# Activation slices of 256 words instead of 272, each tile starting 48 words into its place

## The chip, the core and the metric

The kernel runs on one core of a Trainium2 chip. The core has a matrix engine (TensorE: PE in the profile, with its weight loads listed apart as PEld), a vector engine (DVE), a scalar engine (ACT), GpSimd (POOL) and a queue engine (SP) that issues most of the DMAs. The metric is the device time of one execution in microseconds, as the median of several runs. TensorE's granted clock has two levels, 1.2 and 2.4 GHz, which the profile gives as a share (1.00 is 2.4 GHz).

## The reference

Two transformer-like blocks over 256 tokens of width 1024, in float32. Cut to the large products that matter here:

```python
# first block, 256 tokens
z = rmsnorm(x, g) @ w_in                     # q, k, mq, u (feature-major), v, f, gate (token-major)
x = x + rmsnorm(concat(gmlp, fox, memory) @ w_out, g2)
f = square(relu(rmsnorm(x, g3) @ w_ff1)) @ w_ff2          # 1024 -> 4096 -> 1024
x = x + rmsnorm(f, g4)
# second block, 16 meta tokens + 256 tokens
proj = rmsnorm(h) @ w_in_2                   # z, xbc, dt, conf
h = h + concat(y_ssd, y_conf) @ w_out_2
xt = rmsnorm(h, g5)                          # PEER: 16384 experts
q = xt @ w_query                             # top-16 experts of 8 heads per token
act = gelu(einsum("td,thkd->thk", xt, w_down[experts])) * gate
h = h + einsum("thk,thkd->td", act, w_up[experts])
```

## The kernel before

**Products.** A float32 product is made of three matmuls. `load_split` (line 198) brings a 512 KB piece of weights into `wf` (128 partitions by 1024 words, a DMA on SP's queue), ACT rounds it to `wh` (line 217), and DVE writes the rest, `wl = wf - wh` (line 218). There are four `wf` buffers and three each of `wh` and `wl`. The activations are split in the same way into a pair `..h`, `..l`. `mm3` (lines 221 to 224) then issues, for a weight slice of 128 words and an activation slice:

```python
matmul(o, wh, ah)    # L222
matmul(o, wh, al)    # L223
matmul(o, wl, ah)    # L224
```

In `proj_fm`, `proj_fm_k` and the stage called S below, the weight slice is the stationary operand (128 columns, loaded by PEld), and the activation slice is the moving operand: 256 words, one for each token. While a moving operand streams, PEld loads the weights of the next matmul.

**Where the activations lie.** `act_pair` (line 383) hands out a pair from two places that the whole program shares, tags `acth` and `actl`. It lays a tile out as 8 slices (one for each 128 features) of 272 words, because one stage (`u`, 16 meta tokens and 256 tokens) needs 272; the other stages use the first 256 words of each slice:

- `hh, hl` (line 418): the input of the first block. Moving in the products `qk` and `u` (264 matmuls of 256 words); stationary in the first, token-major product (96 matmuls), in which the weights move.
- `h2h, h2l` (line 772): the input of `w_ff1`, 768 matmuls. They come in 8 groups of 96: 8 slices, and 12 matmuls for each slice. Between two such groups stand 96 matmuls of `w_ff2`, whose activations `fah, fal` come from another pool, with slices of 256 words.
- `uh, ul` (line 882): 272 words, the only user that asks for TM.
- `os1h, os1l` (line 1174): four slices of `w_out_2`'s input, 96 matmuls, 24 for each slice.
- `xth, xtl` (line 1287): the input of the stage S (`w_down`, PEER's first product): 128 steps, each of one 512 KB piece of weights, 8 slices, 3 matmuls for each slice: 3,072 matmuls.

**Addresses.** The built program puts `acth` at byte 61984 and `actl` at 70688 of each partition, the `wh` buffers at 37408, 41504 and 45600, the `wl` buffers at 49696, 53792 and 57888. All six weight buffers start at the same place modulo 512 bytes, and their slices are 512 bytes (128 words) apart. In this document the *distance* of an activation slice is its address minus that of a weight slice, in words, modulo 128. For a user of `act_pair` slice k has the distance 16k: 0, 16, 32, 48, 64, 80, 96, 112, and the `l` tile has the same distances as the `h` tile. `fah, fal` and `os0h, os0l` have 112 in every slice, `xuh, xul` (the input of `w_query`, products `q`) 64 in every slice.

**What sets the order.** The Python order of the code, with generators (`ch`, `bg`) that put attention, selection and gate work between the weight pieces by a budget of estimated microseconds. While S runs, DVE selects the experts (`select`, budget 1.21 for each piece), POOL scatters the gates of the first 128 tokens to DRAM (`scatter`, line 1350, 128 indirect DMAs) and reads them back (line 1522), and later PE puts the gates of the other 128 tokens between S's steps (products `pg`, line 1476). The last stage, `acc` (line 1568, 1,536 matmuls with 512 moving words), uses no `act_pair` tile; DVE's first use of the gates that POOL read back is line 1507.

Of the kernel before, what the change touches and what calls it, by code (L numbers as in the profile page):

```python
# [8 lines left out]
F32R = mybir.dt.float32r  # L9
# [7 lines left out]
P = 128  # L17
T = 256
TM = 272
# [50 lines left out]
LN_WAIT = 1.5, 3.0  # L70

LAST = 3

UP_EARLY = 2

# [83 lines left out]
def tile_two_blocks(ctx: ExitStack, tc: tile.TileContext, A, out):  # L159
# [221 lines left out]
    act = ctx.enter_context(tc.tile_pool(name="act", bufs=1))  # L381

    def act_pair(name, t):
        h = act.tile([P, 8, TM], F32R, name=f"{name}h", tag="acth")
        l = act.tile([P, 8, TM], F32R, name=f"{name}l", tag="actl")
        return h[:, :, :t], l[:, :, :t]

    sres = ExitStack()
    resid = sres.enter_context(tc.tile_pool(name="resid", bufs=1))
# [26 lines left out]

    m0 = xp.tile([P, 8, T], F32, name="m0", tag="x1")
    hh, hl = act_pair("h", T)
    sq = ap.tile([P, 8, T], F32, name="sq", tag="sq")
    mh = ap.tile([P, 8, T], F32R, name="mh")  # L420
# [291 lines left out]
    for k0 in range(0, 8, 2):  # L712
        wh, wl = load_split(A["w_kv"][:, k0:k0 + 2, :], [P, 2, 512])
        for j in range(2):
            k = k0 + j
# [21 lines left out]
    def add_normed(bs, gain, src, dst, eps, name, pool, tmp, then):  # L737

        with tc.high_priority(offset=PRIO):
# [21 lines left out]
            for m in range(8):  # L761
# [8 lines left out]
    assert not zero_parts  # L770
    x1 = xp.tile([P, 8, T], F32, name="x1", tag="x1")
    h2h, h2l = act_pair("h2", T)
    add_normed(bs, "post_mix", x0, x1, eps1, "pm", xp, tp,
               lambda m: split_to(h2h[:, m, :], h2l[:, m, :], x1[:, m, :], col("pre_ffn", m)))
# [16 lines left out]
    for r in range(4):  # L791
        for g in range(4):
            o = _COL["ccw"]
# [55 lines left out]
    for g in range(9):  # L849
# [21 lines left out]
        if g >= 1:  # L871
            ah, al = held[g - 1]
            for j in range(4):
                k = (g - 1) * 4 + j
# [5 lines left out]
                bg.run(BUDGET["diag"])  # L880
    bg.drain()
    uh, ul = act_pair("u", TM)

    split_to(uh[:, :, 0:NM], ul[:, :, 0:NM], meq)
# [632 lines left out]
    for i in range(0, P, 2):  # L1517
# [13 lines left out]
        n = state["toks"]  # L1531
# [20 lines left out]
    for i in range(P):  # L1552
# [11 lines left out]
        def products(t, fs, i=i, ah=ah, al=al, wh=wh, wl=wl):  # L1564
            c = slice(t * P, (t + 1) * P)
            for l, w, e in ((ah, wh, False), (ah, wl, False), (al, wh, i == P - 1)):
                for f in fs:
                    nc.tensor.matmul(acc[t][f], l[:, c], w[:, f * 512:(f + 1) * 512], start=False, stop=e,  # L1568
                                     skip_group_check=True)

        products(0, (0, 1))
        if i >= P - LAST:
            late.append(products)
# [111 lines left out]
```

## Time and profile before

| | us |
|---|---|
| median of 3 runs | 1368.78 |
| lowest and highest run | 1365.6, 1371.24 |
| the profiled execution, whole time | 1370.11 |
| the profiled execution, its span | 1368.4 |

The span is the time from the first to the last instruction of the profile; 1.7 us of the execution lie outside it. PE is busy in 99% of the span, but a busy PE is not a PE at its peak: matmuls overlap, and what counts is the distance in time between the starts of two of them. A matmul of 256 moving words is listed with some 280 ns, while the next one starts some 118 ns later. So the views that matter are the timeline of PE, read by start times, and the list of waits, for what else could hold PE up.

### The profile page before, as it was taken

What the parts mean: (1) busy time and instruction counts of PE and PEld (TensorE: products, weight loads), DVE (VectorE), ACT (ScalarE), POOL (GpSimd) and SP (SyncE); (2) the same over time, 40 slices, a digit from 0 to 9 for tenths busy, and PEclk for the clock granted to TensorE, in tenths of its full rate; (3) what the DMA queues carried; (4) which work ended last, traced back from release to release, by engine and by line L of the source; (5) the groups of instructions that cost most, each with busy time, mean ns of one, the idle gap of its engine ahead of it and who ended that gap; (6) DMA issues with size and microseconds to landing.
All of it is one profiled execution on the core that took longest, in us unless ns stands there. A gap on an engine that the chain in (4) does not pass through costs nothing.

```text
span 1368.4 us, 25834 instructions
## 1 busy us (share of the span) xinstructions
PE 1350.3 (99%) x10054; PEld 1255.6 (92%) x10054; DVE 985.9 (72%) x1924; ACT 756.3 (55%) x1263; POOL 307.1 (22%) x223
## 2 busy tenths in 40 slices
PE   9999999999999999999999999999999999999998
PEld 8988899999888899999999999999998888888886
DVE  6985777657637896798989976666666666666665
ACT  6665444445334675654544548787755555555454
POOL 3122200000310000000048888888600000000000
PEclk9999999999999999999999999999999999999999
DMA  8466666663663343645668776666666777677764
GB/s 297 141 220 226 185 185 189 194 189 113 202 195 107 108 141 109 200 143 165 185 184 186 186 186 156 159 151 158 172 201 220 212 224 220 216 218 214 221 210 131
DMA packets 120730, 250.45 MB, mean 183 GB/s; under 512 B 28048, under 2 KB 52368, under 8 KB 120480
## 3 DMA queue, kind: packets, MB, share of 16 engines
q1 hardware_dynamic: 97328, 235.89, 56.3%
q0 software_dynamic: 22704, 12.35, 6.3%
q8 instruction: 79, 1.29, 0.4%
q10 hardware_dynamic: 576, 0.57, 0.1%
q14 instruction: 43, 0.35, 0.1%
HBM read 234.60 MB, written 9.50 MB: 178 GB/s over the span
## 4 chain that ended last, share of the span: by engine, by line
PE 93%; DVE 3%; DMA 2%; ACT 1%; issue 1%; POOL 0%; SPq 0%; DVEq 0%; ACTq 0%; POOLq 0%
PE acc L1568 25%; PE S L224 9%; PE S L223 9%; PE S L222 9%; PE ff L222 4%; PE ff L223 4%; PE ff L224 4%; PE pg L1476 2%; PE cv L922 2%; PE wo L222 2%; PE wo L224 2%; PE wo L223 2%; PE cf L222 1%; PE cf L224 1%; PE cf L223 1%; PE q L223 1%
## 5 line engine op out<-in xcount | busy, mean ns | idle before, releaser
L218 DVE TENSOR_TENSOR wl<-wf,wh 128x1024 fp32r<-128x1024 f32 (+1 forms) x425 | 515.7, 1215 | 234.7 <-ACT wh L217 234.1
L217 ACT CAST wh<-wf 128x1024 fp32r<-128x1024 f32 (+1 forms) x425 | 442.8, 1043 | 377.9 <-PE S L223 145.4
L222 PE MATMUL S<-xth,wh 128*128 128x256 f32 x1024 | 289.6, 283 | 0.0
L223 PE MATMUL S<-xtl,wh 128*128 128x256 f32 x1024 | 288.6, 282 | 0.0
L224 PE MATMUL S<-xth,wl 128*128 128x256 f32 x1024 | 288.3, 282 | 0.0
L1350 POOL DMA_INDIRECT G<-small x128 | 241.9, 1890 | 163.4 <-DVE small L1344 124.7
L224 PEld LDWEIGHTS S<-xth,wl 128*128 128x128 f32 x1024 | 194.2, 190 | 0.0
L222 PEld LDWEIGHTS S<-xth,wh 128*128 128x128 f32 x1024 | 193.8, 189 | 0.0
L223 PEld LDWEIGHTS S<-xtl,wh 128*128 128x128 f32 x1024 | 192.5, 188 | 0.0
L1568 PE MATMUL acc<-wh,ah 128*128 128x512 f32 x512 | 158.3, 389 | 0.0
L1568 PE MATMUL acc<-wl,ah 128*128 128x512 f32 x512 | 158.2, 389 | 0.0
L1568 PE MATMUL acc<-wh,al 128*128 128x512 f32 x512 | 158.1, 389 | 0.0
L348 ACT CAST ah<-AT 128x256 fp32r<-128x256 f32 x126 | 50.9, 404 | 116.4 <-DVE wl L218 114.3
L1568 PEld LDWEIGHTS acc<-wl,ah 128*128 128x128 f32 x512 | 96.2, 188 | 19.9
L1568 PEld LDWEIGHTS acc<-wh,al 128*128 128x128 f32 x512 | 96.2, 188 | 19.8
L1568 PEld LDWEIGHTS acc<-wh,ah 128*128 128x128 f32 x512 | 96.1, 188 | 19.8
L222 PE MATMUL ff<-h2h,wh 128*128 128x256 f32 x256 | 73.1, 287 | 1.0 <-ACT wh L217 0.6
L222 PE MATMUL ff<-fah,wh 128*128 128x256 f32 x256 | 71.3, 280 | 1.7 <-ACT fah L348 1.7
L223 PE MATMUL ff<-h2l,wh 128*128 128x256 f32 x256 | 72.7, 284 | 0.0
L223 PE MATMUL ff<-fal,wh 128*128 128x256 f32 x256 | 71.6, 280 | 1.1 <-DVE fal L349 1.1
L224 PE MATMUL ff<-h2h,wl 128*128 128x256 f32 x256 | 72.2, 284 | 0.4 <-DVE wl L218 0.4
L349 DVE TENSOR_TENSOR al<-AT,ah 128x256 fp32r<-128x256 f32 x126 | 53.4, 424 | 26.2 <-ACT ah L348 26.2
(501 smaller groups left out, 2691.6 us busy)
## 6 DMA issues: line engine op xcount, KB each, us to landing
wf<-in_wd_dram SPq DMA_DIRECT2D x128, 512.0 KB, 3.7
wf<-in_wu_dram SPq DMA_DIRECT2D x128, 512.0 KB, 3.6
wf<-in_w_ff_dram SPq DMA_DIRECT2D x64, 512.0 KB, 4.2
wf<-in_w_out_dram SPq DMA_DIRECT2D x24, 512.0 KB, 3.6
G<-zg POOLq DMA_DIRECT2D x16, 512.0 KB
wf<-in_w_conf_dram SPq DMA_DIRECT2D x16, 512.0 KB, 3.8
wf<-in_w_xbc_dram SPq DMA_DIRECT2D x16, 512.0 KB, 5.0
wf<-in_w_q_dram SPq DMA_DIRECT2D x16, 512.0 KB, 3.7
```

Source lines behind the costliest of these rows:

```text
L217: nc.scalar.copy(wh[:, :n], wf[:, :n])
L218: nc.vector.tensor_sub(wl[:, :n], wf[:, :n], wh[:, :n])
L222: nc.tensor.matmul(o, lh, rh, start=start, stop=False, skip_group_check=True)
L223: nc.tensor.matmul(o, lh, rl, start=False, stop=False, skip_group_check=True)
L224: nc.tensor.matmul(o, ll, rh, start=False, stop=stop, skip_group_check=True)
L348: nc.scalar.copy(dh, src)
L349: nc.vector.tensor_sub(dl, src, dh)
L922: nc.tensor.matmul(pcv[32 * g:32 * g + 32, i, :], taps[:, m, g, q, :], r4[:, i, g, 4 * q:4 * q + T], start=(i == 0 and q == 0), stop=(q == ...
L1350: s = nc.gpsimd.indirect_dma_start(out=G0, out_offset=bass.IndirectOffsetOnAxis(ap=idx[:, c:c + 1], axis=0), in_=gv[:, c:c + 1], in_offset ...
L1476: nc.tensor.matmul(pg[:, i, :], oh[:, i, :], og[:, i, :], start=True, stop=True, skip_group_check=True)
L1568: nc.tensor.matmul(acc[t][f], l[:, c], w[:, f * 512:(f + 1) * 512], start=False, stop=e, skip_group_check=True)
```

## The change

Tiles of 256 tokens get slices of 256 words and start 48 words into their place; the tile of 272 stays as it was.

```diff
+PHASE = 48
...
     def act_pair(name, t):
-        h = act.tile([P, 8, TM], F32R, name=f"{name}h", tag="acth")
-        l = act.tile([P, 8, TM], F32R, name=f"{name}l", tag="actl")
-        return h[:, :, :t], l[:, :, :t]
+        h = act.tile([P, 8 * TM], F32R, name=f"{name}h", tag="acth")
+        l = act.tile([P, 8 * TM], F32R, name=f"{name}l", tag="actl")
+        o, n = (PHASE, T) if t == T else (0, TM)
+        return [x[:, o:o + 8 * n].rearrange("p (k t) -> p k t", k=8) for x in (h, l)]
```

(`T` is 256, `TM` 272.) Every buffer of the program keeps its address, and every engine has the same instructions in the same order with the same waits; only the addresses of the slices inside `hh, hl`, `h2h, h2l`, `os1h, os1l` and `xth, xtl` move. With slices of 1024 bytes, a multiple of 512, each of them now has the distance 48 from the weights, in the `h` and the `l` tile alike.

## Rows read from the trace of the kernel before

**Rows 1.** The page's head, and its chain that ended last.

```profile
span 1368.4 us, 25834 instructions
...
PE 1350.3 (99%) x10054; PEld 1255.6 (92%) x10054; DVE 985.9 (72%) x1924; ACT 756.3 (55%) x1263; POOL 307.1 (22%) x223
...
PE acc L1568 25%; PE S L224 9%; PE S L223 9%; PE S L222 9%; PE ff L222 4%; PE ff L223 4%; PE ff L224 4%; PE pg L1476 2%; PE cv L922 2%; PE wo L222 2%; PE wo L224 2%; PE wo L223 2%; PE cf L222 1%; PE cf L224 1%; PE cf L223 1%; PE q L223 1%
```

**Rows 2.** PE's longest wait, whole span: engine, line, releaser; total us, times, longest.

```profile
PE ff L222 <- ACT fah L348: 1.7, 1, 1.7
```

**Rows 3.** Windows: stretch, each engine's busy us (instructions), granted clock, DMA share, GB/s.

```profile
640.00:660.00 20.00, 20.00 (x171) 20.00 (x171) 19.38 (x62) 9.44 (x12) 0.00 (x0) 1.00 0.61 187
...
720.00:740.00 20.00, 20.00 (x171) 20.00 (x170) 19.29 (x60) 8.85 (x10) 17.25 (x10) 1.00 0.79 188
740.00:760.00 20.00, 20.00 (x171) 20.00 (x170) 18.95 (x58) 9.34 (x11) 17.26 (x10) 1.00 0.83 189
760.00:780.00 20.00, 20.00 (x171) 20.00 (x170) 19.32 (x62) 9.91 (x11) 17.26 (x10) 1.00 0.78 185
```

**Rows 4.** PE's timeline (start, us, line, product), os1's slices 0 to 3, and the end.

```profile
550.34 0.28 PE L222 MATMUL wo<-os1h,wh 128*128 128x256 f32 x1
...
553.22 0.28 PE L222 MATMUL wo<-os1h,wh 128*128 128x256 f32 x1
...
556.05 0.28 PE L222 MATMUL wo<-os1h,wh 128*128 128x256 f32 x1
...
558.89 0.28 PE L222 MATMUL wo<-os1h,wh 128*128 128x256 f32 x1
...
561.62 0.47 PE L222 MATMUL q<-xuh,wh 128*128 128x256 f32 x2
```

**Rows 5.** PE's timeline, one group of w_ff2, then one of w_ff1 (its slice 7 last).

```profile
182.65 0.28 PE L222 MATMUL ff<-fah,wh 128*128 128x256 f32 x1
...
193.53 0.28 PE L222 MATMUL ff<-h2h,wh 128*128 128x256 f32 x1
...
203.44 0.28 PE L222 MATMUL ff<-h2h,wh 128*128 128x256 f32 x1
...
203.79 0.29 PE L222 MATMUL ff<-h2h,wh 128*128 128x256 f32 x1
...
204.14 0.28 PE L222 MATMUL ff<-h2h,wh 128*128 128x256 f32 x1
...
204.82 0.28 PE L222 MATMUL ff<-fah,wh 128*128 128x256 f32 x1
```

**Rows 6.** PE's timeline, w_query's product, two matmuls 54 apart.

```profile
593.85 0.28 PE L222 MATMUL q<-xuh,wh 128*128 128x256 f32 x1
...
600.33 0.28 PE L222 MATMUL q<-xuh,wh 128*128 128x256 f32 x1
```

**Rows 7.** PE's timeline, one step of S: slice 0, slice 3, slice 4, the next step's slice 0.

```profile
701.11 0.28 PE L222 MATMUL S<-xth,wh 128*128 128x256 f32 x1
...
702.17 0.28 PE L222 MATMUL S<-xth,wh 128*128 128x256 f32 x1
...
702.53 0.28 PE L222 MATMUL S<-xth,wh 128*128 128x256 f32 x1
...
703.95 0.28 PE L222 MATMUL S<-xth,wh 128*128 128x256 f32 x1
```

**Rows 8.** The tile xth: matmuls, min/median/max ns, first and last start.

```profile
L222 PE MATMUL S<-xth,wh x1024: 276/280/367, 621.5 to 1013.9; 128*128 128x256 f32 x171
```

**Rows 9.** Pieces of the chain that ended last: start, us, what.

```profile
904.67 0.89 PE pg L1476 x8
...
1014.47 348.22 PE acc L1568 x1536
```

**Rows 10.** DVE's waits from 640 to 830 us.

```profile
DVE wl L218 <- ACT wh L217: 19.4, 25, 1.6
```

**Rows 11.** POOL's timeline, its last scatter and the reads that follow.

```profile
977.94 1.55 POOL L1350 DMA_INDIRECT G<-small  x1 [0.30 <-issue]
982.84 1.62 POOL L1522 DMA_DIRECT2D small<-G  x2 [3.34 <-issue]
```

**Rows 12.** DVE's timeline, its first use of what these reads bring.

```profile
1011.27 0.29 DVE L1507 TENSOR_TENSOR AT<-AT,small 128x128 f32<-128x128 f32 x1
```

## The prediction

> **What bounds the kernel now.** I first read the page's head and its chain. PE is busy for 99% of the span, and the chain that ended last runs through PE almost everywhere; the stage S has 27% of it, the last stage 25%, `w_ff1` and `w_ff2` together 12% [rows 1]. I then looked for what holds PE up: the longest wait in the whole span is 1.7 us, and no matmul of S is in the list [rows 2]. So an engine that is never fed late sets the time, and the question is how fast one matmul follows another. The clock can't improve: it is granted at 1.00 in these stretches [rows 3].
>
> The third view is PE's timeline, read by start times. All matmuls compared here have the same shape: 128 by 128 weights, 256 moving words. They don't follow each other at the same rate:
>
> - S: 24 matmuls from 701.11 to 703.95, 2.84 us, 118.3 ns each [rows 7].
> - `w_ff1`: 96 from 193.53 to 204.82, 11.29 us, 117.6 ns [rows 5].
> - `w_ff2`: 96 from 182.65 to 193.53, 10.88 us, 113.3 ns [rows 5].
> - `w_query`: 54 from 593.85 to 600.33, 6.48 us, 120.0 ns [rows 6].
>
> The first two have eight distances in turn, `w_ff2` has 112 throughout, `w_query` 64 throughout. The decisive rows are os1's. There one loop runs over four slices of one tile, with 24 matmuls for each slice, the same weight buffers and the same outputs. Slice 0 (distance 0) takes 2.88 us, slice 1 (16) 2.83, slice 2 (32) 2.84, slice 3 (48) 2.73, or 113.8 ns a matmul to the rounding of the view [rows 4]. Within one group of `w_ff1` the same shows at slice 7 (distance 112): its first three matmuls take 0.35 us, the next three 0.35, the last six 0.68, or 113.3 ns each [rows 5]. So at 48 and at 112 PE settles at 113.3 ns after about six matmuls, and at the other distances it stays near 118 to 120. In S a slice has only three matmuls: slice 3 runs from 702.17 to 702.53, 120 ns each, although its distance is 48 [rows 7]. PE leaves the slice before it settles.
>
> **The change part by part.** It moves no instruction and no wait. It gives each slice of four tiles the distance 48, the one that os1's slice 3 has now. What a matmul costs there I take from `w_ff2`, 113.3 ns, since it is measured over 96 matmuls; os1's slice 3 agrees.
>
> *S.* A step goes from 2.84 us to 24 x 113.3 ns = 2.72. Over 128 steps that is 0.12 x 128 = 15.4 us. Some 35 interruptions (mostly `pg` products like the one at 904.67, [rows 9]) each cost the settling again, as slice 7 of `w_ff1` shows: 0.70 us for six instead of 0.68, so 0.02 us; together 0.7 at most, of which I take 0.4. That leaves 15.0 us. Does everything else keep up with 2.72 us a step? For the weights the last stage answers: 348.22 us over 128 pieces of the same 512 KB is 2.72 us a piece, with the same DMA, ACT and DVE work for each [rows 9], and PE doesn't wait there. DVE is closer. While it selects experts it is busy for 57.6 of the 60 us from 720 to 780, and 19.4 of 20 from 640 to 660 [rows 3]. The work that PE does in 60 us will take it 57.5, so DVE has no room left in those 80 us. What covers it is the three buffers: DVE's waits for `wh` in 640 to 830, 19.4 us in 25 times, are the moments at which all of them were full and it had nothing to do [rows 10]; 67 steps need 8.0 us less, and 19.4 are there. Where a stretch has no such wait, DVE may fall behind by what it lacks there, with its gaps between instructions some 1 to 2 us in 60, and it starts up to a step ahead. I take 0. Without that cover all the gain of those 80 us would be lost, 80 x 0.12 / 2.84 = 3.4 us.
>
> POOL's scatter doesn't get faster. Its last instruction starts at 977.94, the reads go out at 982.84 [rows 11], and DVE wants them at 1011.27 [rows 12]: 26 us later from the end of their issue (984.46), of which the landing needs a few. S ends 15 us earlier against its own start, and the scatter's start comes forward by 77 us x 0.12 / 2.84 = 3.3, so the margin shrinks by 12 us and stays positive. Cost 0.
>
> *`w_ff1`.* A group goes from 11.29 to 10.88 us: 0.41 for each of the seven groups that run undisturbed, 2.9, and 0.2 for the first, in which PE waits between matmuls: 3.1 us.
>
> *`qk` and `u`.* 264 matmuls at `w_ff1`'s mixture: at most 264 x 4.3 ns = 1.1 us, at least 0 if the attention work between them takes over. I take 0.5.
>
> *os1.* 2.88 + 2.83 + 2.84 + 2.73 = 11.28 us becomes 10.88: 0.4 us.
>
> *The first product*, in which `hh, hl` are the weights: 96 matmuls while PE waits for its first loads. The spread between the best and the poorest rate, 120.0 - 113.3 = 6.7 ns, bounds it at 0.6 us either way; I take 0.
>
> The sum is 15.0 + 3.1 + 0.5 + 0.4 = 19.0 us. The span goes from 1368.4 to 1349.4, the profiled execution's 1370.11 to 1351.1. The median of the runs lies 1.3 us below that execution, so I expect 1368.78 - 19.0 = **1350 us**, 1.4% less.
>
> **The rivals.** A measurement here tells about 0.5% (7 us) from no change.
>
> *No change, 1369.* The address isn't the cause: something that goes along with it is. Then S stays at 118.3 ns, and the other three with it. The rule for this stands in the Trainium skill, "SBUF — State Buffer", section "Who interferes with whom": the matrix engine has one read port for the moving operand and an independent one for weight loads, and never waits for anyone; where a slice lies would not matter. Against it stand the four slices of os1, which differ in nothing but the address and take 2.73 to 2.88 us [rows 4]. For it: in S no row shows the settled rate, and its 24 matmuls in a row into one output have no example at 113 ns. 6%.
>
> *Each new slice starts over, 1361.* If the settling belongs to the change of slice and not to the change of distance, S never gets past the first three matmuls: 0.35 us for three, 116.7 ns [rows 5], a gain of 1.6 ns x 3,072 = 5 us, and some 2 in the other stages, where a slice has 12 or 24. Against it: `w_ff2` changes its slice every 24 matmuls, and 96 of them still take 113.3 ns each [rows 5]. 4%.
>
> *DVE becomes the bound while it selects, 1354.* The mechanism and its price, 3.4 us, are above. It decides once DVE lacks more in a stretch than the buffers hold. 9%.
>
> *Slower, 1377.* One distance for all slices can also lock PE into the poor rate: `w_query` at 64 stays at 120.0 ns and never leaves it [rows 6], while eight distances in turn average 118.3. If 48 behaves in S as its slice 3 does now (120 ns, [rows 7]), S loses 1.7 x 3,072 = 5.2 us and the other 1,128 matmuls 2.4 ns each, 2.7: 1377. It decides above the present 118.3 ns. Against it: 48 is the distance of os1's fast slice. 3%.
>
> **How the numbers follow.** The forecast gets 78%. The range takes in DVE as the bound, the first product and `qk` either way (0.6 each), and the runs' own spread of 2.8 us around their median: 1345 to 1357. Outside stay the other three rivals, 13%, and some of the cases' edges. Faster by over 0.5% (below 1362): the forecast, DVE's case and half of "starts over", 89%. Within 0.5%: no change and the other half, 8%. Slower: 3%.
>
> **What would show it.** In the profile after: a step of S takes 2.72 us on PE's timeline and S 15 us less than the 392 from its first to its last start [rows 8]; a group of `w_ff1` takes 10.88 us; os1's four slices are alike; `w_query` and `w_ff2` are unchanged; DVE's waits for `wh` in the selection shrink from 19.4 us to some 11; no matmul of S waits for `wl`. Waits of S for `wl` between 640 and 780 would mean DVE's case; 116.7 ns in S the case of starting over; 118 or more would mean that the distance is not what sets the rate, and the prediction is wrong at its root.

## The result, and the profile after

The kernel with the change takes 1353.62 us (median of four runs, 1352.36 to 1354.17), the kernel before beside it 1369.24: a ratio of 0.9893, interval 0.9869 to 0.9918. That is 15.6 us less, where the forecast said 19 less, and 1353.6 lies inside its range. The profiled execution took 1354.1 us. The same program measured a second time, on another occasion, took 1358.32 (ratio 0.9921, 0.9891 to 0.9951), a little above the range, and that difference turned out to be the more interesting half of the case.

The head and the chain of the page after, against [rows 1]:

```profile
span 1352.4 us, 25834 instructions
...
PE 1332.2 (99%) x10054; PEld 1237.4 (91%) x10054; DVE 983.7 (73%) x1924; ACT 756.0 (56%) x1263; POOL 297.6 (22%) x223
...
PE acc L1571 26%; PE S L226 9%; PE S L225 9%; PE S L224 9%; PE ff L225 4%; PE ff L226 4%; PE ff L224 4%; PE pg L1479 2%; PE cv L925 2%; PE wo L224 2%; PE wo L226 2%; PE wo L225 2%; PE cf L224 1%; PE cf L226 1%; PE cf L225 1%; PE q L225 1%
```

(Lines stand two or three further down than before: S's are now L224 to L226, `pg` is L1479, `acc` L1571.) The counts are the same, PE is still busy in 99% of the span, and the chain still runs through it. What shrank is PE's own busy time, by 18.1 us: the matmuls follow one another faster. The tile `xth`, against [rows 8]:

```profile
L224 PE MATMUL S<-xth,wh x1024: 276/276/369, 616.9 to 998.0; 128*128 128x256 f32 x171
```

S takes 381.1 us from its first to its last start in this row, 392.4 before. One step, on PE's timeline (start, us, line, product), against [rows 7]:

```profile
701.35 0.28 PE L224 MATMUL S<-xth,wh 128*128 128x256 f32 x1
...
704.07 0.28 PE L224 MATMUL S<-xth,wh 128*128 128x256 f32 x1
```

The 24 matmuls take 2.72 us instead of 2.84: 113.3 ns each, as forecast. A group of `w_ff1`, 96 matmuls, against [rows 5]:

```profile
192.79 0.28 PE L224 MATMUL ff<-h2h,wh 128*128 128x256 f32 x1
...
203.67 0.28 PE L224 MATMUL ff<-fah,wh 128*128 128x256 f32 x1
```

10.88 us instead of 11.29, 113.3 ns each. But os1, against [rows 4]:

```profile
545.84 0.28 PE L224 MATMUL wo<-os1h,wh 128*128 128x256 f32 x1
...
557.14 0.40 PE L224 MATMUL q<-xuh,wh 128*128 128x256 f32 x2
```

11.30 us for 96 matmuls, 117.7 ns each, as slow as before, although all four slices now have the distance 48 at which slice 3 took 113.8 before. The same shows in the second half of S, where the gate products `pg` stand between the steps:

```profile
843.63 0.36 PE L224 MATMUL S<-xth,wh 128*128 128x256 f32 x1
843.83 0.28 PE L225 MATMUL S<-xtl,wh 128*128 128x256 f32 x1
...
846.42 0.28 PE L226 MATMUL S<-xth,wl 128*128 128x256 f32 x1
846.54 1.06 PE L1479 MATMUL pg<-og,oh 128*128 128x128 f32 x8
847.36 0.37 PE L224 MATMUL S<-xth,wh 128*128 128x256 f32 x1
847.56 0.28 PE L225 MATMUL S<-xtl,wh 128*128 128x256 f32 x1
...
850.06 0.28 PE L226 MATMUL S<-xth,wl 128*128 128x256 f32 x1
...
852.90 1.05 PE L1479 MATMUL pg<-og,oh 128*128 128x128 f32 x8
...
853.91 0.28 PE L225 MATMUL S<-xtl,wh 128*128 128x256 f32 x1
...
856.50 0.28 PE L226 MATMUL S<-xth,wl 128*128 128x256 f32 x1
```

Same code, same distance, nothing waited for: in the first step 22 gaps between starts take 2.59 us (843.83 to 846.42, 117.7 ns each), in the second 2.50 (847.56 to 850.06, 113.6 ns with its settling), and in the step after the next `pg` 2.59 again (853.91 to 856.50). So at the distance 48 PE has **two rhythms**, 113.3 and 117.8 ns, and which one it runs in changes at an interruption. Step by step through S: in its quiet part (the first 68 steps; the first interruption comes after 72) all 68 run at 113.3 ns, 118.3 before. In its gate part (the other 60) 26 run at 113 to 114, and 34 at 117.8.

The order of these is not a mixture by chance. S has 33 interruptions in this trace (32 of eight `pg` matmuls, and ahead of them one of three matmuls called `pj`), and each of them turns the rhythm over: 17 times from the fast to the slow one, 16 times back. Where one step follows another with nothing between, 94 times, the rhythm stays. So of the 34 slow steps 17 follow an interruption, and 17 took the slow rhythm over from the step before them.

DVE's waits from 636 to 826 us, against [rows 10], and PE's longest waits, against [rows 2] (us in total, times, longest):

```profile
DVE wl L220 <- ACT wh L219: 13.5, 14, 1.5
```

```profile
PE ff L224 <- ACT fah L350: 1.9, 1, 1.9
...
PE qk L226 <- DVE wl L220: 1.4, 2, 0.9
```

DVE used up some of its spare waits (19.4 before), and no matmul of S waits for `wl`.

By the starts of the stages the 16.0 us of the span went so:

| stretch | before, us | after, us | change | forecast |
|---|---|---|---|---|
| start to the end of the first products | 65.2 | 65.5 | +0.2 | -0.5 |
| from there to `w_ff1` | 62.0 | 62.7 | +0.6 | 0 |
| `w_ff1` and `w_ff2` | 195.3 | 191.6 | -3.7 | -3.1 |
| second block's first products (nothing of it touched) | 177.0 | 175.3 | -1.7 | 0 |
| `w_out_2`, os1 in it | 62.1 | 62.2 | 0.0 | -0.4 |
| `w_query` | 59.9 | 59.8 | -0.1 | 0 |
| S | 392.8 | 381.4 | -11.4 | -15.0 |
| the last stage | 348.0 | 348.0 | 0.0 | 0 |

### The profile page after: what moved, and what is told of

The parts are those of the page before. It is cut to its first block, busy times and chain, and to the rows that moved or that the text cites. A ratio compares the mean times of both kernels' runs of the same rounds, so it can differ in the third digit from the quotient of the medians.

```text
span 1352.4 us, 25834 instructions
## 1 busy us (share of the span) xinstructions
PE 1332.2 (99%) x10054; PEld 1237.4 (91%) x10054; DVE 983.7 (73%) x1924; ACT 756.0 (56%) x1263; POOL 297.6 (22%) x223
## 4 chain that ended last, share of the span: by engine, by line
PE 91%; DVE 3%; DMA 2%; ACT 2%; issue 1%; POOL 0%; SPq 0%; ACTq 0%; DVEq 0%; POOLq 0%
PE acc L1571 26%; PE S L226 9%; PE S L225 9%; PE S L224 9%; PE ff L225 4%; PE ff L226 4%; PE ff L224 4%; PE pg L1479 2%; PE cv L925 2%; PE wo L224 2%; PE wo L226 2%; PE wo L225 2%; PE cf L224 1%; PE cf L226 1%; PE cf L225 1%; PE q L225 1%
## 5 line engine op out<-in xcount | busy, mean ns | idle before, releaser
L224 PE MATMUL S<-xth,wh 128*128 128x256 f32 x1024 | 287.0, 280 | 0.0
L225 PE MATMUL S<-xtl,wh 128*128 128x256 f32 x1024 | 284.1, 277 | 0.0
L226 PE MATMUL S<-xth,wl 128*128 128x256 f32 x1024 | 284.0, 277 | 0.0
L1353 POOL DMA_INDIRECT G<-small x128 | 233.9, 1827 | 160.4 <-DVE small L1347 121.7
L224 PEld LDWEIGHTS S<-xth,wh 128*128 128x128 f32 x1024 | 192.4, 188 | 0.0
L226 PEld LDWEIGHTS S<-xth,wl 128*128 128x128 f32 x1024 | 192.2, 188 | 0.0
L1571 PE MATMUL acc<-wh,ah 128*128 128x512 f32 x512 | 158.2, 389 | 0.0
L1571 PE MATMUL acc<-wl,ah 128*128 128x512 f32 x512 | 158.1, 389 | 0.0
L1571 PE MATMUL acc<-wh,al 128*128 128x512 f32 x512 | 158.0, 389 | 0.0
L1571 PEld LDWEIGHTS acc<-wl,ah 128*128 128x128 f32 x512 | 96.1, 188 | 20.0
L1571 PEld LDWEIGHTS acc<-wh,al 128*128 128x128 f32 x512 | 96.1, 188 | 19.8
L1571 PEld LDWEIGHTS acc<-wh,ah 128*128 128x128 f32 x512 | 96.1, 188 | 19.9
L224 PE MATMUL ff<-fah,wh 128*128 128x256 f32 x256 | 71.0, 279 | 1.9 <-ACT fah L350 1.9
L224 PE MATMUL ff<-h2h,wh 128*128 128x256 f32 x256 | 71.6, 281 | 0.8 <-ACT wh L219 0.6
L226 PE MATMUL ff<-fah,wl 128*128 128x256 f32 x256 | 71.4, 279 | 0.0
```

The lines of the kernel that those rows point to most:

```text
L224: nc.tensor.matmul(o, lh, rh, start=start, stop=False, skip_group_check=True)
L225: nc.tensor.matmul(o, lh, rl, start=False, stop=False, skip_group_check=True)
L226: nc.tensor.matmul(o, ll, rh, start=False, stop=stop, skip_group_check=True)
L1353: s = nc.gpsimd.indirect_dma_start(out=G0, out_offset=bass.IndirectOffsetOnAxis(ap=idx[:, c:c + 1], axis=0), in_=gv[:, c:c + 1], in_offset ...
```

## The experiments

Two questions: is it the distance that sets the rate (or something that goes along with it), and what decides between the two rhythms at one distance? The mean gaps below are means over the starts of neighbouring matmuls on PE's timeline, without those over 160 ns (interruptions). All diffs are against the changed kernel. The kernel before, measured beside each of these, took 1365.7 to 1368.9 us, and each ratio is to the one beside it; so kernels are compared by the ratios rather than by the microseconds. The expectations set the theories against one another in numbers; behind each stands what held and what fell.

**The same kernel again.** No edit.

> The changed kernel once more, on the chip of the three that follow, so that they can be set beside it: 0.989 of the kernel before, S's quiet part (its first 68 steps, before the gate products begin) at 2.72 us a step, since PE entered S in the fast rhythm in all runs so far.

Four runs: 1360.91 (the profiled one), 1358.04, 1358.61 and 1352.9; median 1358.32, ratio 0.9921 (0.9891 to 0.9951). In this profile all 68 quiet steps take 117.8 ns, while os1 takes 113.3. The expectation, S entered in the fast rhythm in all runs, fell. So one and the same program enters S in either rhythm from one execution to the next, and that is worth 7.7 us of S (389.0 from first to last start instead of 381.3).

**Other distances, 0 and 112.**

```diff
-PHASE = 48
+PHASE = 0
```

> One part of the change alone: slices of 256 words, so one distance for all, but that distance is 0 (the tile starts at the start of its place). Theory A, the distance sets the rate: a step of S takes what w_query's product takes at distance 64, 24 x 120.0 ns = 2.88 us (between 2.83 and 2.88 if 0 and 64 are not alike), and the whole is no faster than the kernel before: 1369 to 1377 us. Rival B, slices of 1024 bytes are what helps and their start is of no account: a step takes 2.72 us in the quiet part of S, and the whole is the changed kernel's 1353.6 us.

1371.34 us, ratio 1.0049 (1.0034 to 1.0063): slower than the kernel before. The quiet steps take 120.0 ns each, the gate steps 119.8, S 397.5 us. The one distance that `w_query` had shown [rows 6] (64 there) costs the same here. So the slices of 256 words as such bring nothing; where they lie does.

```diff
-PHASE = 48
+PHASE = 112
```

> The changed kernel with its start moved by a further 64 words, to the distance 112 that w_ff2's activations have. Theory A with a pattern that repeats every 64 words: a step of S takes 2.72 us in the quiet part, and the whole is within 3 us of the changed kernel's 1353.6 us. Rival C, what counts is the distance in a longer pattern, or the place in the partition itself: another rate in S, and a time apart from 1353.6 by more than 5 us. Where PE falls into the slower of its two rhythms (117.8 ns) after the gate products may differ, which is worth up to 4 us either way.

1360.02 us, ratio 0.9954 (0.9934 to 0.9974), six runs within 1.2 us of each other. At 112, where `w_ff2` averages 113.4 ns in the kernel before, S's quiet steps all take 117.8. The expected 2.72 us a step fell, and by the time alone rival C would have won. But 23 of the gate steps run at 113 to 114 ns here as well, and two kernels below run the quiet part at 113.3 at this very distance. So the second rhythm belongs to both distances, and here the program enters S in it every time, as far as the times of the six runs tell.

The windows of these kernels (stretch; busy us and instructions of PE, PEld, DVE, ACT, POOL; granted clock; DMA share; GB/s), 100 us of the quiet part. The first is before:

```profile
640.00:740.00 100.00, 100.00 (x847) 100.00 (x847) 90.19 (x222) 48.35 (x56) 35.66 (x19) 1.00 0.67 187
```

The kernel after, first measurement:

```profile
640.00:740.00 100.00, 100.00 (x885) 100.00 (x884) 92.83 (x229) 50.60 (x59) 41.99 (x23) 1.00 0.74 191
```

The kernel after, second measurement:

```profile
640.00:740.00 100.00, 100.00 (x851) 100.00 (x851) 90.57 (x224) 48.46 (x56) 40.51 (x22) 1.00 0.71 185
```

Distance 0:

```profile
640.00:740.00 100.00, 100.00 (x836) 100.00 (x835) 89.15 (x216) 47.98 (x55) 35.59 (x18) 1.00 0.65 184
```

Distance 112:

```profile
640.00:740.00 100.00, 100.00 (x851) 100.00 (x851) 90.57 (x223) 48.12 (x56) 40.86 (x22) 1.00 0.66 186
```

The count in the first bracket is the rate: 885 matmuls in 100 us are 113 ns each, 851 are 117.5, 836 are 119.6 (two or three only overlap the edges). The clock is 1.00 and PE is busy for the whole 100 us in all five, so neither the clock nor the busy share tells them apart. DVE is busiest (92.83) where PE is fastest: it follows PE, not the other way round.

**All distances in one run.** Two measuring kernels go through 16 distances, 0 to 60 words in steps of 4, each for 96 matmuls of S: one in rising, one in falling order. The weight buffers get room for the offset, which costs one of the four `wf` buffers; the moving operand of the last stage is shifted in the same manner.

```diff
+SCAN = [0, 4, 8, 12, 16, 20, 24, 28, 32, 36, 40, 44, 48, 52, 56, 60]
...
-        wh = wpool.tile([P, 1024], F32R, tag="wh", name=f"wh{cnt[0]}")
-        wl = wpool.tile([P, 1024], F32R, tag="wl", name=f"wl{cnt[0]}")
+        wh = wpool.tile([P, 1152], F32R, tag="wh", name=f"wh{cnt[0]}")
+        wl = wpool.tile([P, 1152], F32R, tag="wl", name=f"wl{cnt[0]}")
...
-            wh, wl = load_split(A["wd"][i + e], [P, 8, P])
+            wh, wl = load_split(A["wd"][i + e], [P, 8, P], (PHASE - SCAN[(i + e) // 4 % len(SCAN)]) % 64)
```

(`load_split` writes and hands out its tiles from that offset on; the other order has the list reversed.)

> A measuring kernel, not a faster one: the weight slices of S start 0 to 60 words later in their buffers, so that the distance of its activations goes 0, 4, 8, ... 60 and over again, four steps (96 matmuls) at each; in the last stage the stationary slices move likewise, four rows (48 matmuls of 512 words) at each distance. It has three wf buffers instead of four to make room, so the early stages may be slower; only the rates in S and in the last stage are read. Theory A: the rate in S is a function of the distance, 113.3 ns around 48, near 118 to 120 at 0, 16 and 32, as the slices of the kernel before show; the distances between are new. In the last stage, at distance 0 before (226.7 ns), some distances give up to 5 or 10 ns less if the same thing acts on matmuls of 512 words, and 226.7 throughout if not. Rival B, the distance is of no account: all rates alike.

> The same measuring kernel with the distances in falling order, 60, 56, ... 0. Theory A with two rhythms that PE keeps until something disturbs it: at some distances, 48 among them, the rate depends on the distance that came before, and differs from that of the rising order (113.3 in one, 117.8 in the other). If the rate is a function of the distance alone, both orders give the same rate at each distance to within 0.5 ns.

One run each, 1380.56 and 1376.38 us. The last stage has its share in that: its 1,536 matmuls of 512 words are pushed off their distance 0 too, which at some 5 ns each is 8 us. The rates, second half of each 96 matmuls of S's quiet part, ns:

| distance mod 64 | rising | falling | | distance | rising | falling |
|---|---|---|---|---|---|---|
| 0 | 120.0 | 120.0 | | 32 | 118.5 | 118.7 |
| 4 | 119.9 | 120.0 | | 36 | 120.0 | 120.0 |
| 8 | 116.7 | 116.7 | | 40 | 118.8 | 118.6 |
| 12 | 116.6 | 116.7 | | 44 | 118.7 | 118.8 |
| 16 | 117.8 | 117.8 | | 48 | **117.8** | **113.4** |
| 20 | 118.0 | 118.1 | | 52 | 118.3 | 117.8 |
| 24 | 120.0 | 119.9 | | 56 | 118.4 | 118.3 |
| 28 | 120.0 | 118.3 | | 60 | 118.3 | 118.3 |

Fourteen of the sixteen agree to 0.5 ns in both orders, within one program and with the same work around. In the scan the weights are moved, in the kernels with another PHASE the activations; 0 gives 120.0 ns both ways, and 48 gives 113.3 or 117.8. The distance between the two sets the rate: that point is settled. The exceptions are 28 and 48. At 48, coming from 44 it is 117.8 ns, coming from 52 it is 113.4. 48 is the only place of the sixteen with a rate under 116 ns. For the last stage the same scan gives 226.7 to 227.0 ns at 0 and 4, and 229 to 234.5 everywhere else (227.0 once at 60, in the second falling pass): the kernel's own distance there, 0, is already the best.

**What S is entered from.** The scan suggested that the distance just before decides. Three kernels put twelve matmuls of another distance ahead of S's first step; they write into an output that the step then overwrites.

```diff
+            if i + e == 0:
+                other = places["xt"][:, PHASE + 4:PHASE + 4 + T]
+                for _ in range(12):
+                    nc.tensor.matmul(S[:, 0, :], wh[:, 0, :], other, start=True, stop=True, skip_group_check=True)
```

(`places["xt"]` is the whole tile behind `xth`.) With PHASE 112 and `other` four words further (52 mod 64):

> The kernel with start 112, in which S's quiet part ran at 117.8 ns a matmul, with one thing added: before the first step of S twelve more matmuls, whose moving operand lies at distance 116 (the scan in falling order went from there into 113.3 ns); their result is overwritten. Theory A2, at 48 and 112 PE has two settled rhythms, 113.3 and 117.8 ns, and keeps the one in which it enters: S's quiet part now runs at 113.3 ns, 68 steps x 0.107 us = 7.3 us less, 1.4 us more for the twelve: 5.9 us below the 0.9954 of the kernel with start 112, so 0.991 of the kernel before. Rival D, 112 is a poorer place for S than 48, whatever PE did before: S's quiet part stays at 117.8 ns, and the whole is 1.4 us longer than with start 112 (0.996 to 0.997).

1356.19 us, ratio 0.9913 (0.9877 to 0.9948), but in two groups: 1352.99 and 1351.95, 1361.49 and 1359.39. In the profile the quiet steps average 113.35 ns. (The median meets the expected 0.991 by chance: no run lies near it.) Next to distance 112 without the twelve matmuls, which took 1359.4 to 1360.6 in six of six runs, the entry does decide; but this entry decides it only in some executions. (The two slower runs have no trace. That they ran at 117.8 ns is read from their time alone.)

With PHASE 48 and `other` at 44, the order that gave 117.8 ns in the scan:

> The mirror of the kernel with start 112 and twelve matmuls: the changed kernel (start 48), and before the first step of S twelve matmuls at distance 44, from which the scan in rising order went into 117.8 ns. Theory A2: S's quiet part runs at 117.8 ns, 7.3 us more and 1.4 for the twelve: 8.7 us above the changed kernel, 0.995 to 0.996 of the kernel before. Rival D: S's quiet part stays at 113.3 ns, and the whole is 1.4 us above the changed kernel.

1352.91 us, ratio 0.9887 (0.9861 to 0.9913), 113.34 ns in the quiet part. A miss: 44 ahead of 48 doesn't force the slow rhythm. So the distance before is not enough to tell.

With PHASE 112 and `other` at 32 mod 64. In the kernel before, all 21 stretches at 48 or 112 that followed on 32 or 96 had settled at 113.3:

> The kernel with start 112, which ran S's quiet part at 117.8 ns in every execution (six runs at 1359.4 to 1360.6 us, before at 1365.7), and twelve matmuls ahead of S at distance 96, which is 32 modulo 64; their result is overwritten. In the kernel before, all 21 stretches at distance 48 or 112 that follow one at 32 or 96 settled at 113.3 ns. Theory A2, the rhythm that PE is in on entering decides: S's quiet part at 113.3 ns in all executions, 0.991 of the kernel before, the runs within 3 us of each other. Rival E, the entry is drawn at random whatever ran before: the runs fall into two groups 7 us apart, as those of the changed kernel did in its second measurement (1352.9 and 1358.0 to 1360.9).

1351.65 us, ratio 0.989 (0.9871 to 0.9908); six runs from 1350.60 to 1354.15, none in the upper group. Against the same kernel without the twelve matmuls (1360.02, ratio 0.9954) that is 8.4 us less for twelve matmuls more. The entry alone moved S from 389.0 to 380.0 us.

**The other tiles too.** `xuh` (distance 64 before) and `och` (96) are moved to 112:

```diff
-            och = bp.tile([P, 8, T], F32R, name="och", tag="h0")
+            och = bp.tile([P, 16 + 8 * T], F32R, name="och", tag="h0")[:, 16:].rearrange("p (k t) -> p k t", k=8)
...
-    xuh = qp.tile([P, 8, T], F32R, name="xuh")
-    xul = qp.tile([P, 8, T], F32R, name="xul")
+    def at(pool, name, o, **how):
+        return pool.tile([P, o + 8 * T], F32R, name=name, **how)[:, o:].rearrange("p (k t) -> p k t", k=8)
+
+    xuh = at(qp, "xuh", 48)
+    xul = at(qp, "xul", 0)
```

> The changed kernel with two more tiles at the distance 48 modulo 64: w_query's input from 64 to 112 (384 matmuls, 119.8 ns now) and the h half of one input of w_out_2 from 96 to 112 (the l half is at 112 already; 192 matmuls, 119.2 ns now). If PE enters the fast rhythm there: 384 x 6.5 + 192 x 5.9 = 3.6 us less than the changed kernel. If it enters the slow one: 384 x 2.0 + 192 x 1.4 = 1.0 us less. The rest as in the changed kernel, unless the other entry changes the rhythm in which S begins, which would cost 7.3 us.

1350.73 us, ratio 0.9872 (0.9847 to 0.9898). `w_query`'s mean gap goes from 119.7 to 116.2 ns (48.4 to 47.5 us), the product from `och` from 119.1 to 114.8 (24.3 to 23.6). Together that is 1.6 us, between the two expected sums (1.0 and 3.6): among `w_query`'s gaps there are now both kinds, 113 to 114 and 117 to 118 ns, and these stages have interruptions too.

**Both together.** These tiles and, at PHASE 48, the twelve matmuls at 32:

> The changed kernel with w_query's input and the h half of w_out_2's input at 112 as well, and the twelve matmuls at a distance of 32 modulo 64 ahead of S. Theory A2: S's quiet part at 113.3 ns in all executions, so no run in the upper group; 1.4 us for the twelve against the kernel without them where that enters fast (0.9872), so 0.988 of the kernel before. Rival E: a part of the runs 7 us above the rest.

1359.43 us, ratio 0.994 (0.9922 to 0.9957), six runs from 1357.7 to 1360.0. A clear miss: all 68 quiet steps at 117.8 ns, six times of six. What had worked at 112 failed at 48. PE's timeline at the entry of S (L1540 are the twelve, of which the stretch shown has the last ten):

```profile
613.96 1.35 PE L1540 MATMUL S<-xth,wh 128*128 128x256 f32 x10
615.15 0.28 PE L224 MATMUL S<-xth,wh 128*128 128x256 f32 x1
...
617.98 0.28 PE L224 MATMUL S<-xth,wh 128*128 128x256 f32 x1
```

The first step takes 2.83 us. Read gap by gap, the twelve themselves don't run at one rate: at the distance 32 the gaps go round in fives, 115, 117 to 118, 122, 120, 119 ns. The last gaps of the twelve, then the first of S:

```
twelve at 32, then 112 (settles):        ... 115 118 122 | 118 117 115 115 113 113
twelve at 32, then 48 (does not settle): ... 122 120 119 115 | 118 119 117 119 117 118
```

The round had come to another place when the distance changed. If that place decides, three matmuls fewer should be able to turn the result over.

**Nine instead of twelve.**

```diff
-                for _ in range(12):
+                for _ in range(9):
```

> The kernel before this one in the list (all tiles at 48 or 112, twelve matmuls at 32 modulo 64 ahead of S) with nine of these instead of twelve, and nothing else. At the distance 32 the gaps between PE's matmuls go round in fives, 115, 117 to 118, 122, 120, 119 ns. With twelve, the last gap was 115 in the kernel that then stayed at 117.8 ns, and 122 in the one that went to 113.3. Nine end at the 122. Theory A3, the place in this round at which the distance changes decides: S's quiet part at 113.3 ns in all executions, 7.3 + 0.35 us less than with twelve, 0.988 to 0.989 of the kernel before. Rival E, drawn at random or set by the program ahead of S: S's quiet part stays at 117.8 ns (0.994), or the runs fall into two groups.

1350.56 us, ratio 0.9874 (0.985 to 0.9897); five runs from 1349.97 to 1352.38. The quiet part averages 113.34 ns; its first step takes 113.8, the other 67 take 113.3. (Of the nine, the stretch shown has the last six.)

```profile
613.97 0.88 PE L1540 MATMUL S<-xth,wh 128*128 128x256 f32 x6
614.68 0.28 PE L224 MATMUL S<-xth,wh 128*128 128x256 f32 x1
...
617.42 0.28 PE L224 MATMUL S<-xth,wh 128*128 128x256 f32 x1
```

The first step takes 2.74 us with its settling, the gaps being 120 119 115 118 121 at the end of the nine and then 119 116 116 114 114 113. Three matmuls fewer, 8.9 us less, five runs of five against six of six. The kernel before bears the place out: its 21 stretches that settled after 32 or 96 had left that distance after a gap of 120 ns (17 times), 119 (twice) or 117 (twice), never after the 115. The windows say the same, twelve first:

```profile
640.00:740.00 100.00, 100.00 (x852) 100.00 (x851) 90.54 (x224) 48.48 (x56) 41.53 (x22) 1.00 0.71 187
```

and nine:

```profile
640.00:740.00 100.00, 100.00 (x885) 100.00 (x884) 92.78 (x233) 50.11 (x59) 44.02 (x24) 1.00 0.73 191
```

**What stands before a gate step.** The operands of `pg`, `og` and `oh`, are moved by 48 words (both alike, so their distance from each other stays), with the last stage kept at its distance 0 (and `w_query`'s tile at 112 as a side effect):

```diff
+    gpad = sp.enter_context(tc.tile_pool(name="gpad", bufs=1)).tile([P, 48], F32, name="gpad")
...
-        ah = up.tile([P, T], F32R, tag="oh", name=f"ah{i}")
-        al = up.tile([P, T], F32R, tag="og", name=f"al{i}")
+        ah = up.tile([P, 320], F32R, tag="oh", name=f"ah{i}")[:, 16:16 + T]
+        al = up.tile([P, 320], F32R, tag="og", name=f"al{i}")[:, 16:16 + T]
```

> The changed kernel with the operands of the gate products pg moved by 48 words (the last stage's operands keep their distance, w_query's input goes to 112). It asks about the other half of S, in which pg breaks in after two of every three steps: there 34 to 37 of 60 steps ran at 117.8 ns. If what PE did just before decides, the share of slow steps changes (to anything from 0 to 60, worth 2.6 us a twenty-four of them); if pg's own place is of no account, 34 to 37 of 60 stay slow. The time of the whole also depends on the rhythm in which S begins, so S's steps are read, not the total.

1353.27 us, ratio 0.9902 (0.9879 to 0.9925). The quiet part is at 113.34 ns, but of the 60 gate steps 54 now run at the slow rhythm and 5 at the fast one (34 and 26 in the kernel after); the sixtieth changes on its way. The 5 all lie ahead of the first `pg`. Where in the kernel after each interruption turned the rhythm over, here PE is in the slow one after each of the 32 `pg`, whichever it ran in before. The windows from 830 to 930, this kernel first:

```profile
830.00:930.00 100.00, 100.00 (x859) 100.00 (x859) 67.48 (x145) 79.51 (x203) 85.06 (x50) 1.00 0.69 155
```

and the kernel after:

```profile
830.00:930.00 100.00, 100.00 (x870) 100.00 (x869) 68.10 (x146) 79.45 (x203) 85.11 (x49) 1.00 0.69 156
```

870 matmuls against 859. The steps of S themselves lie where they lay; only what runs just before them has other addresses, and more of them stay in the slow rhythm. So the interruptions do what the twelve matmuls do at the entry. They were moved the wrong way here; a place that helps wasn't looked for.

All of them side by side (S from its first to its last start; the first four of the 60 gate steps lie ahead of the first interruption):

| kernel | us | ratio to before | quiet step, ns | gate steps at 113-114 / 117.8 | S, us |
|---|---|---|---|---|---|
| before | 1369.24 | 1 | 118.3 | mean 118.4 | 392.7 |
| after | 1353.62 | 0.9893 | 113.3 | 26 / 34 | 381.3 |
| after, again | 1358.32 | 0.9921 | 117.8 | 23 / 37 | 389.0 |
| distance 0 | 1371.34 | 1.0049 | 120.0 | mean 119.8 | 397.5 |
| distance 112 | 1360.02 | 0.9954 | 117.8 | 23 / 37 | 389.0 |
| 112, twelve at 52 | 1356.19 | 0.9913 | 113.3 | 37 / 23 | 380.0 |
| 48, twelve at 44 | 1352.91 | 0.9887 | 113.3 | 37 / 23 | 380.0 |
| 112, twelve at 32 | 1351.65 | 0.989 | 113.3 | 37 / 23 | 380.0 |
| other tiles at 112 | 1350.73 | 0.9872 | 113.3 | 26 / 34 | 381.3 |
| that, twelve at 32 | 1359.43 | 0.994 | 117.8 | 23 / 37 | 388.9 |
| that, nine at 32 | 1350.56 | 0.9874 | 113.3 | 37 / 23 | 380.0 |
| `pg` moved | 1353.27 | 0.9902 | 113.3 | 5 / 54 | 383.3 |

The best are the other tiles at 112 and the same with nine matmuls ahead of S: 18.2 and 16.3 us less than the kernel before beside them. By the ratios that is some 3 us less than the change, though their intervals overlap with the change's.

## Why the prediction was right, and where it wasn't

**The cause was right.** PE was never fed late, and one matmul following another at a rate that the address sets was the matter. The four slices of os1 [rows 4] had shown it rightly: the scan and the distances 0, 48 and 112 show that the distance sets the rate, up to the choice between the two rhythms (1.0049 against 0.9893 with one constant changed). The rule of the Trainium skill ("SBUF — State Buffer", section "Who interferes with whom"), that the matrix engine's two read ports are independent and it waits for nobody, read as the rival *No change* reads it, would have given 1369 for every distance. The runs go against that reading of it: 120.0 ns at the distance 0, and 113.3 or 117.8 at 48 and 112, for the same shapes in the same program with only the address changed.

**S, forecast -15.0, measured -11.4.** This is the term that was mis-sized, and the failing step is the sentence that each interruption "costs the settling again", 0.02 us, of which 0.4 us was taken in all. It costs the settling only if PE settles. After 17 of the 33 interruptions it went into 117.8 ns and stayed there until the next one, 34 steps in all: 34 x 24 x 4.45 ns = 3.6 us, which is what is missing. Since each interruption turned the rhythm over, PE was in the slow one for over half of the gate part. Slice 7 of `w_ff1` [rows 5] was one example of settling, and I had taken it for the rule. A contrary sign was in the trace of before: os0, whose four slices have the distance 112 as `fah` has, averaged 115.9 ns beside `w_ff2`'s 113.4, with 48 of its matmuls at 117.8. They follow an interruption by eight matmuls (`pby`), and the 45 gaps from 545.04 to 550.34 take 5.30 us:

```profile
543.80 1.05 PE L1198 MATMUL pby<-cst,rc_y 128*128 128x128 f32 x8
...
545.04 0.28 PE L222 MATMUL wo<-os0h,wh 128*128 128x256 f32 x1
...
550.34 0.28 PE L222 MATMUL wo<-os1h,wh 128*128 128x256 f32 x1
```

I had read `w_ff2`, the long and undisturbed one, and not os0.

**The same blind spot is behind the second measurement.** A rate that follows from the distance alone can't give 1353.6 and 1358.3 for one program. Where S is entered in the slow rhythm, its 72 steps ahead of the first interruption keep it: 72 x 24 x 4.45 = 7.7 us, by which S differs. The forecast's range, 1345 to 1357, held no case for it, and three of the four runs of the second measurement (1358.0 to 1360.9) lie outside it.

**`w_ff1`, forecast -3.1, measured -3.7 with `w_ff2`.** A group takes 10.88 us, to the hundredth what was forecast. The rest can't be told from scatter: traces with the same distances modulo 64 give 189.3 to 193.3 us for the stage.

**`qk` and `u` (0.5), os1 (0.4).** The first can't be read: the stretch up to the end of the first products takes 64.1 to 65.9 us over the traces (those of the scan, with three `wf` buffers, left out), 65.5 here. os1 didn't come for the same reason as in S: it was entered in the slow rhythm, in which os0 had ended, and kept it for all 96. In the second measurement, and with nine matmuls, os1 took 10.9 us, 0.4 less, as forecast.

**-1.7 us in the second block's first products,** in which nothing was changed, was not forecast. The changed kernels take 173.7 to 175.3 us there (those of the scan left out), and the one trace of the kernel before, 177.0, lies above them all. The kernel at distance 0 takes 175.3 too, so the rates are not behind it; whether the new layout is, or the scatter of one trace, isn't shown.

**The rivals.** *No change* fell (0.9893). *Each slice starts over* fell: a quiet step takes 2.72 us with eight slices, not 116.7 ns a matmul. *DVE as the bound* fell: its waits shrank from 19.4 to 13.5 us (some 11 were forecast), and no matmul of S waited; the three buffers covered it as argued. *Slower* fell, but its mechanism is real: at the distance 0 S is locked into 120.0 ns, and the kernel is slower than before; my price for it was 1377, the measured 1371.3 beside a before of 1365.7 is 5.6 more instead of 8. POOL's margin and the last stage (348.0 us, unchanged) cost nothing, as forecast. (POOL's margin before was 26.8 us by [rows 11] and [rows 12], not 26, which changes nothing.)

**What stays open.** Which memory or port conflict makes the rates and the two rhythms wasn't tried, and nothing here shows it. That the place in the round decides rests on one kernel for the slow side (twelve ahead of 48, the change after the 115) against the 21 stretches of the kernel before and two kernels for the fast side. Nine and twelve were measured on two chips on two occasions, and since the unchanged kernel too entered S otherwise on another occasion, a part of the occasion in it isn't ruled out. Why this place, and why each `pg` turns the rhythm over, isn't shown. Why one unchanged program enters S now in one rhythm, now in the other isn't settled; that the few ns by which matmuls ahead of S are late shift that place would fit, but it was only argued.

## What to carry to other kernels

Where PE is the bound, compare the gaps between starts of equal matmuls across stages of the same trace before looking at waits: a few ns of difference with nothing waited for point to where the operands lie, and one constant can be worth over 1%. Look also at short and interrupted stretches before taking the rate of a long one for all: the same address can have two steady rates. A steady rate once entered lasts until something interrupts, so count the interruptions of a stage and look at which rate follows each of them; and where the time falls into two groups, look at the last dozen matmuls ahead of the longest stretch.

## What the runs showed of the hardware

- Matmuls of 128 by 128 weights and 256 moving words, with the weights of the next one loaded meanwhile, follow at 113.3 to 120.0 ns by the distance of moving operand and weights (table of the scan), the clock at 1.00 in these stretches; 0 and 64 words agree, and so do 48 and 112. Two of sixteen distances, 28 and 48, gave another rate in the other order. With 512 moving words it is 226.7 ns at the distance 0 and up to 234.5 elsewhere, while 0 is among the worst for 256.
- At the distances 48 and 112 there are two steady rhythms, 113.3 and 117.8 ns. PE keeps the one it entered for as long as nothing comes between: 72 steps, 1,728 matmuls, in each of the ten traces with S at one of these distances. Eight `pg` matmuls turn it over, 32 times of 32 in the kernel after and 31 of 32 in its second measurement; with `pg`'s operands 48 words further they leave PE in the slow one every time.
- It isn't load that makes the slow one: the last 7 steps of S (979 to 998 us), with no gate work left, stay at 117.8 ns, while the quiet part with DVE at its busiest (92.8 of 100 us) runs at 113.3, and the same 7 steps do in the kernel with nine matmuls.
- Nine matmuls instead of twelve ahead of 3,072 others changed the kernel by 8.9 us.
